# Low parts of layer 0's weights and the sums of squares on VectorE in place of GpSimd, and the first norm's products in another order

## The chip, the cores and the metric

The kernel runs on one core of one Trainium2 chip. The metric is the device time of one execution in microseconds (us); three executions of the kernel before give a median, and one further execution was profiled. The engines are named as in the profile: PE is TensorE, DVE is VectorE, ACT is ScalarE, POOL is GpSimd, SP is SyncE, which issues most DMAs.

## What is computed

A two-layer transformer block on 512 latent tokens and 256 context tokens, 1024 wide, all in float32. Layer 0 mixes with a gated linear recurrence (RG-LRU), layer 1 with a latent attention (MLA); each layer has a SwiGLU feed-forward part of hidden width 2816. Each part is entered through an RMS norm with a shift and a scale (and left through a gate) that are made from the conditioning vector.

```python
def _rmsnorm(x, g):
    y = xf * lax.rsqrt(jnp.mean(xf * xf, axis=-1, keepdims=True) + NORM_EPS)
...
def _modulate(h, shift, scale):
    return h * (1.0 + scale) + shift
...
def _swiglu(h, w_in, w_out):
    g, u = jnp.split(h @ w_in, 2, axis=-1)
    return (jax.nn.silu(g) * u) @ w_out
...
def _rglru_mixer(h_ctx, h_lat, w_in, conv_w, conv_b, gate_w, gate_b, lam, w_out, need_ctx):
    g_lat, u_lat = jnp.split(h_lat @ w_in, 2, axis=-1)
    u_lat = _dwconv_centred(u_lat, conv_w, conv_b)
    ...
    a_l, b_l = _rglru_coeffs(u_lat, gate_w[d], gate_b[d], lam[d])
    hl, _ = _linear_scan(a_l, b_l, hc_final, reverse)
    out_lat = ((y_lat[0] + y_lat[1]) * jax.nn.gelu(g_lat)) @ w_out
```

## The kernel before

**Two-part products.** Every float32 operand of a matmul is split into a high part in a rounded format and the low remainder. A product is then three matmuls, high by high, low by high and high by low (`mm3`, L791). Activations are kept transposed, features on partitions: `xT` is the residual stream, `hh` and `hl` the two parts of the normed input. `LAT` is columns 0 to 511, `CTXS` columns 512 to 767.

**The weight stream.** `Stream` brings the weights in. SP loads a raw tile of 1 or 0.5 MB (`raw`, two buffers, `NB_RAW = 2`); ACT makes the high part `wh` from it (L108), and the engine `st.low_engine` then makes the low part, `wl = raw - wh` (L119). In the code `advance` emits L108 of a unit, and emits L119 of the unit before it (`flush` emits what is left). When the last L119 of a raw tile has been emitted, `fill` emits the next load into the same buffer, so on the chip that load waits for this L119. `low_engine` is POOL from the start through the LRU, DVE in layer 0's feed-forward part, POOL from that part's last output tiles on and in the MLA, DVE in layer 1's feed-forward part and POOL for its entry.

**The start** (`START`, L38) is an order written out by hand. `h0` splits unit 0, `H` flushes, `B` and `D` turn bias rows into columns, `S`, `E` and `L` are products, evacuations and loads for the conditioning, `n` and `l` make the first norm's `nt`/`hh` (L669, L671) and `hl` (L672), `pkj` are PE's three matmuls of row k with weight unit j.

**The LRU.** For four blocks: a convolution (ACT L895, then DVE L899 twelve times for two tiles), its split (ACT `uh` L904, DVE `ul` L905), gate products on PE (`ga`), tanh on ACT (`tg` L931), the decay and scan on DVE (L941 to L964), the gated result's split (L985, L988) and the out product (`lo`). Each stage is in order on its engine. The L119 of the weights to come stand among them on POOL. POOL also issues the loads of the conditioning weights (`ada`, L242), which wait for PE.

**Boundaries.** Four times the residual is updated from PSUM by DVE (`xT`, L767) for eight row blocks m, and the sum of squares of the new `xT` is collected: ACT squares it (`sq`, L783) and POOL adds it (`acc`, L785), deferred in the list `accs`. Context columns come first, then latent columns; while the latent blocks are updated, the context blocks are normed (`nt`, `hh`, `hl`) and PE multiplies them with the next part's weights. Boundary 1 stands between LRU and feed-forward part (about 343 to 375 us), 2 before the MLA (870 to 925), 3 before layer 1's feed-forward part (1170 to 1200), 4 is the end.

Of the kernel before, what the change touches and what calls it, by code (L numbers as in the profile page):

```python
# [12 lines left out]
ALU = mybir.AluOpType  # L13
# [3 lines left out]
D = 1024  # L17
# [18 lines left out]
ENTRY_AT = (12, 6)  # L36

START = (  # L38
    "H h0 L1 S00 X S01 S02 Y B S03 E0 h1 n0 l0 n1 h2 D S10 H l1 S11 S12 p01 S13 p00 L2 p10 E1 p11 n2 "
    "l2 S20 p02 p12 C S21 n3 S22 S23 l3 p20 p21 E2 n4 p22 p31 p30 l4 p32 n5 L3 S30 l5 A S31 S32 S33 "  # L40
    "p41 E3 n6 p40 l6 p42 p52 p51 p61 n7 p50 l7 C p60 p70 h3 p71 p62 p72 H C").split()

# [19 lines left out]
class Stream:  # L62
# [3 lines left out]
    def __init__(self, nc, raw_pool, w_pool):  # L66
        self.nc, self.raw_pool, self.w_pool = nc, raw_pool, w_pool
        self.loads, self.units = [], []
        self.loaded = self.split = self.base = 0
        self.raw, self.tiles, self.freed, self.pending = {}, {}, set(), []  # L70
        self.hold = 0
        self.more = {}
        self.low_engine = nc.gpsimd

    def load(self, cols, emit):
        self.loads.append([cols, emit, 0])
# [69 lines left out]
def kernel(ctx, tc, x, c, ctx_in, c_ctx, ada_w, ada_b, norm_mix_g, norm_ffn_g, ffn_w_in,  # L146
# [3 lines left out]
    nc = tc.nc  # L150
    act, dve, pe = nc.scalar, nc.vector, nc.tensor
# [109 lines left out]
    st = Stream(nc, raw_pool, w_pool)  # L261
# [334 lines left out]
    def ada_until(l, ch):  # L596
        n = sum(1 for a in adas if a[:2] <= (l, ch)) - ada_state["used"]
        for _ in range(n):
            ada_add()
            ada_evac()  # L600
            ada_one()
        if n >= 0:
            ada_add()
            ada_evac()
# [26 lines left out]
    acc = big.tile([P, T], F32, name="acc")  # L631
# [69 lines left out]
    def boundary(last_group, na, after=lambda i: None, at=(1, 3, 2)):  # L701

        n = len(last_group)
        i0, i1, per = (0, 1, 3) if n == 4 else at
        k = 0
        act.activation(ss6[:, 0:1], ones[:, 0:1], AF.Sqrt)
        for i, f in enumerate(last_group):
            f()
            if i == i0:
                na.stats()  # L710
            if i == i1:
                na.spread()
            after(i)
            if i >= i1:
                flush_acc()
                if k < KT:
                    na.tiles(k, min(KT, k + per))
                k = min(KT, k + per)
        if k < KT:
            na.tiles(k, KT)  # L720
# [33 lines left out]
    accs = []  # L754
    sq_from, last_sq = [None], [None]

    def final_gain(m, s):
        dve.tensor_scalar(xT[:, m, s], xT[:, m, s], fin_g[:, m:m + 1], None, op0=ALU.mult)

    def flush_acc():  # L760
        while accs:
            accs.pop(0)()

    def residual(m, ps, l, ch, group, stat):

        v, s = group
        dve.scalar_tensor_tensor(xT[:, m, s], ps(s) if callable(ps) else ps[:, s], mod[:, l, ch, v, m:m + 1], xT[:, m, s],  # L767
                                 op0=ALU.mult, op1=ALU.add)
        flush_acc()
        if stat:  # L770
            at_end = l == 1 and ch == 5 and m == KT - 1 and s.start > 0
            if l == 1 and ch == 5 and not at_end:
                accs.append(lambda: final_gain(m, s))
            if m == 0:
                act.activation(acc[:, s], xT[:, m, s], AF.Square)
            else:
                sq = sq_from[0](f"sq{l}{ch}{m}{s.start}")
                if sq.shape[1] == T:
                    last_sq[0] = sq
                    sq = sq[:, s]  # L780
                else:
                    sq = sq[:, :s.stop - s.start]
                act.activation(sq, xT[:, m, s], AF.Square)  # L783
                if not at_end:
                    accs.append(lambda: nc.gpsimd.tensor_tensor(acc[:, s], acc[:, s], sq, op=ALU.add))  # L785

    def mm3(ps, wh, wl, xh, xl, parts, first, last, off=0):

# [347 lines left out]
    def ffn0(na, nb, nxt):  # L1136
        ga, gb = na.group, nb.group
        with ExitStack() as es:
# [14 lines left out]
            A, B = slice(0, H2), slice(H2, T)  # L1153
# [49 lines left out]
            def out_tile(c, m, groups, ks, ps=None):  # L1203
                h0, nh, outs = s0_out[c]
                per = 8 // nh
                wh, wl = st.get(outs[m // per])
                ps = ps or {g[0]: ps_bank(f"fo0{c}{m}{g[0]}")[:, :g[1].stop - g[1].start] for g in groups}
                for k in ks:
                    o = k * (1024 // nh) + m % per * P
                    for q, (w, x) in enumerate(((wh, ah), (wh, al), (wl, ah))):  # L1210
                        for v, s in groups:
                            pe.matmul(ps[v], w[:, o:o + P], x[:, k, s], start=k == 0 and q == 0,  # L1212
                                      stop=k == nh - 1 and q == 2)
                return ps

            def out_done(c, m):
                per = 8 // s0_out[c][1]
                if m % per == per - 1:
                    st.done(s0_out[c][2][m // per])
# [4 lines left out]
            def pair(j, i, last):  # L1224

                g = tmp.tile([P, T], F32, name=f"g0{j}", tag="nt")
                p5 = ptemp(f"p5{j}")
                y, z, x = (ps_bank(f"{c}{j}")[:, :H2] for c in "yzx")
                product(1, j, x, True, True)
                act.activation(g[:, A], x, AF.Copy)  # L1230
                while split:
                    split.pop()()
                release(1, j)
                ada_step()
                product(5, j, z, True, True)
                act.activation(p5, z, AF.Copy)
                release(5, j)
                product(6, j, x, False, True)
                act.activation(g[:, B], x, AF.Copy)
                release(6, j)  # L1240
                product(2, j, y, True, True)
                dve.tensor_tensor(g[:, A], g[:, A], y, op=ALU.add)
                act.activation(g[:, A], g[:, A], AF.Silu)
                release(2, j)
                if on_pe():
                    ada_step()
                product(7, j, x, False, True)
                dve.tensor_tensor(p5, p5, x, op=ALU.add)
                release(7, j)
                product(3, j, z, False, True)  # L1250
                dve.tensor_tensor(g[:, B], g[:, B], z, op=ALU.add)
                act.activation(g[:, B], g[:, B], AF.Silu)
                release(3, j)
                product(4, j, x, False, True)
                dve.tensor_tensor(g[:, B], g[:, B], p5, op=ALU.mult)
                dve.tensor_tensor(g[:, A], g[:, A], x, op=ALU.mult)
                if last:
                    split_hidden(i, g)
                else:
                    split.append(lambda: split_hidden(i, g))  # L1260
                release(4, j)
# [40 lines left out]
            for c, (h0, nh, outs) in enumerate(s0_out):  # L1302
                for j in range(max(h0, PLAIN0), h0 + nh):
                    pair(j, j - h0, j == h0 + nh - 1)
                lastp = c == len(s0_out) - 1
                if lastp:
                    ada_until(1, 4)
                    for m in range(KT):
                        ps = out_tile(c, m, (ga,), range(nh))
                        residual(m, lambda s: ps[1], 0, 5, ga, True)  # L1310
                        if m == 0:
                            st.flush()
                    st.low_engine = nc.gpsimd

                    def last(m):
                        ps = out_tile(c, m, (gb,), range(nh))
                        residual(m, lambda s: ps[0], 0, 5, gb, True)
                        out_done(c, m)

                    boundary([lambda m=m: last(m) for m in range(KT)], nxt, at=(1, 2, 1))  # L1320
                    return

                n0 = nh - 1 if c else 2
                three = [out_tile(c, m, (gb, ga), range(n0)) for m in range(3)]
                for m in range(KT):
                    if m < 3:
                        ps = out_tile(c, m, (gb, ga), range(n0, nh), three[m])
                    else:
                        ps = out_tile(c, m, (gb, ga), range(nh))
                    for g in (gb, ga):  # L1330
                        residual(m, lambda s: ps[g[0]], 0, 5, g, False)
                    out_done(c, m)
                    ada_step(1 if nh < 4 or on_pe() else 2)
# [3 lines left out]
    adastack.close()  # L1337
    adastack = ExitStack()
    ffn0(na, nb, na1)
    ps_layout((3, 1024))  # L1340
    adastack.close()
# [414 lines left out]
```

## Time and profile before

| what | value |
|---|---|
| three executions | 1569.62, 1568.83, 1565.91 us; median 1568.83 |
| the profiled execution | 1571.79 us, of which the span of the trace is 1569.9 |
| PE busy | 1512.2 us (96%) |
| DVE busy | 934.2 us (60%) |
| ACT busy | 675.9 us (43%) |
| POOL busy | 281.5 us (18%) |

The span runs from the first to the last instruction; what lies around it is 1.9 us. The profiled execution is 2.96 us above the median. A busy time is a sum over instructions and averages over stages with different limits: PE is busy throughout the feed-forward parts, and has gaps in the start, the LRU and at the boundaries.

### The profile page before, as it was taken

The numbers are of one execution on the slowest core, as the hardware profiler recorded it, in microseconds if no ns is written. First come the engines' busy times: TensorE is split into PE (matmuls) and PEld (weight loads), VectorE is DVE, ScalarE is ACT, GpSimd is POOL, SyncE is SP. The second block draws the span as 40 slices with busy tenths as digits, with TensorE's granted clock in tenths as the row PEclk, the third lists the DMA queues.
The fourth block names the chain that finished last, engine by engine and source line by source line (L and its number), as shares of the span: only waits on it lengthen the run. The fifth ranks groups of instructions, "written<-read, shape, count | busy, mean of one in ns | idle before, by whom it ended". The sixth has DMA issues, their size and how long they took to land.

```text
span 1569.9 us, 21629 instructions
## 1 busy us (share of the span) xinstructions
PE 1512.2 (96%) x8903; PEld 1321.4 (84%) x8903; DVE 934.2 (60%) x1397; ACT 675.9 (43%) x989; POOL 281.5 (18%) x261
## 2 busy tenths in 40 slices
PE   7999998979999999999999998999998999999998
PEld 5877876868878898999989887899998888888887
DVE  5766778686855657767587457666537543233234
ACT  5486555734423241433424343766644322232223
POOL 3223333242010101001010332111144100000002
PEclk9999999989999999999999999999999999999999
DMA  9434333131233334333242112110112433223222
GB/s 359 127 108 135 108 122 120 59 103 48 68 108 114 104 112 128 114 114 122 94 141 64 51 56 69 29 43 28 54 54 75 161 118 104 81 98 117 81 69 93
DMA packets 134995, 155.14 MB, mean 99 GB/s; under 512 B 6252, under 2 KB 112353, under 8 KB 134897
## 3 DMA queue, kind: packets, MB, share of 16 engines
q1 hardware_dynamic: 122272, 112.21, 22.3%
q0 software_dynamic: 12320, 41.02, 8.2%
q8 instruction: 70, 1.15, 0.3%
q10 hardware_dynamic: 304, 0.53, 0.1%
q14 instruction: 29, 0.23, 0.0%
HBM read 151.64 MB, written 2.10 MB: 98 GB/s over the span
## 4 chain that ended last, share of the span: by engine, by line
PE 82%; DVE 11%; ACT 4%; issue 1%; DMA 1%; SPq 0%; POOL 0%; DVEq 0%; ACTq 0%; POOLq 0%
PE f L791 14%; PE fo L1212 11%; PE x L1166 10%; PE fo L791 8%; PE z L1166 5%; PE lo L791 3%; PE s L1555 3%; PE ga L791 2%; PE wo L791 2%; PE y L1166 2%; PE o L1597 2%; PE p L791 2%; PE g L791 2%; DVE yc L899 1%; PE t L1573 1%
## 5 line engine op out<-in xcount | busy, mean ns | idle before, releaser
L108 ACT ACTIVATE wh<-raw 128x1024 fp32r<-128x1024 f32 (+3 forms) x247 | 208.5, 871 | 203.9 <-PE fo L1212 64.5
L119 POOL TENSOR_TENSOR wl<-raw,wh 128x1024 fp32r<-128x1024 f32 (+3 forms) x66 | 157.5, 2397 | 328.8 <-ACT wh L108 328.6
L119 DVE TENSOR_TENSOR wl<-raw,wh 128x1024 fp32r<-128x1024 f32 (+2 forms) x181 | 169.3, 948 | 11.8 <-ACT wh L108 11.8
L767 DVE SCALAR_TENSOR_TENSOR xT<-fo,mod,xT 128x512 f32<-128x512 f32 (+1 forms) x124 | 74.1, 626 | 129.8 <-PE fo L1212 66.2
L239 POOL DMA_DIRECT2D ada<-in_ada_w_dram x96 | 51.7, 539 | 465.3 <-PE psada L570 217.9
L791 PE MATMUL f<-hh,wh 128*128 128x512 f32 x320 | 124.7, 390 | 0.0
L791 PE MATMUL f<-hh,wl 128*128 128x512 f32 x320 | 124.5, 389 | 0.0
L791 PE MATMUL f<-hl,wh 128*128 128x512 f32 x320 | 124.5, 389 | 0.0
L785 POOL TENSOR_TENSOR acc<-acc,sq 128x256 f32<-128x256 f32 (+1 forms) x52 | 50.7, 975 | 374.1 <-ACT sq L783 371.9
L1212 PE MATMUL fo<-ah,wh 128*128 128x512 f32 (+1 forms) x352 | 98.3, 345 | 0.9 <-DVE g L1273 0.8
L1212 PE MATMUL fo<-al,wh 128*128 128x512 f32 (+1 forms) x352 | 95.8, 338 | 0.4 <-DVE al L1201 0.4
L1212 PE MATMUL fo<-ah,wl 128*128 128x512 f32 (+1 forms) x352 | 95.3, 337 | 0.0
L1109 DVE TENSOR_TENSOR sg<-sg,f 128x512 f32<-128x512 f32 x20 | 13.7, 687 | 116.4 <-ACT sg L1108 116.4
L1108 ACT ACTIVATE sg<-f 128x512 f32<-128x512 f32 x20 | 12.0, 599 | 148.3 <-PE f L791 148.3
L791 PE MATMUL fo<-ah,wh 128*128 128x512 f32 (+1 forms) x200 | 73.0, 365 | 0.0
L791 PE MATMUL fo<-ah,wl 128*128 128x512 f32 (+1 forms) x200 | 72.7, 364 | 0.0
L791 PE MATMUL fo<-al,wh 128*128 128x512 f32 (+1 forms) x200 | 72.7, 364 | 0.0
L791 PEld LDWEIGHTS f<-hh,wh 128*128 128x128 f32 x320 | 60.1, 188 | 13.2 <-issue 0.8
L791 PEld LDWEIGHTS f<-hh,wl 128*128 128x128 f32 x320 | 60.1, 188 | 12.6
L791 PEld LDWEIGHTS f<-hl,wh 128*128 128x128 f32 x320 | 60.1, 188 | 12.4
L1212 PEld LDWEIGHTS fo<-ah,wh 128*128 128x128 f32 x352 | 56.2, 188 | 12.8 <-issue 4.6
L1212 PEld LDWEIGHTS fo<-al,wh 128*128 128x128 f32 x352 | 56.2, 188 | 8.0 <-DVE al L1201 0.7
(490 smaller groups left out, 4023.3 us busy)
## 6 DMA issues: line engine op xcount, KB each, us to landing
raw<-in_ffn_w_in_dram SPq DMA_DIRECT2D x26, 1024.0 KB, 4.9
ada<-in_ada_w_dram POOLq DMA_DIRECT2D x96, 256.0 KB, 3.1
raw<-in_ffn_w_out_dram SPq DMA_DIRECT2D x19, 1024.0 KB, 4.9
raw<-in_ffn_w_in_dram SPq DMA_DIRECT2D x36, 512.0 KB, 4.7
ada<-in_ada_w_dram POOLq DMA_DIRECT2D x30, 512.0 KB, 4.4
ada<-in_ada_w_dram SPq DMA_DIRECT2D x32, 256.0 KB, 5.5
raw<-in_lru_w_in_dram SPq DMA_DIRECT2D x10, 512.0 KB, 5.3
raw<-in_lru_gate_w_dram SPq DMA_DIRECT2D x16, 256.0 KB, 3.2
```

What stands on the lines that cost most here:

```text
L108: nc.scalar.activation(dst(hi), src(self.raw[load]), AF.Copy)
L119: self.low_engine.tensor_tensor(dst(lo), src(self.raw[load]), dst(hi).bitcast(F32), op=ALU.subtract)
L239: eng.dma_start(t, ada_w[l, k * P:(k + 1) * P, c0:c0 + 512])
L767: dve.scalar_tensor_tensor(xT[:, m, s], ps(s) if callable(ps) else ps[:, s], mod[:, l, ch, v, m:m + 1], xT[:, m, s], op0=ALU.mult, op1=ALU ...
L785: accs.append(lambda: nc.gpsimd.tensor_tensor(acc[:, s], acc[:, s], sq, op=ALU.add))
L791: pe.matmul(ps[:, off + s.start:off + s.stop], a, b[:, s], start=first and i == 0, stop=last and i == 2)
L899: dve.scalar_tensor_tensor(y[:, s0:s1], ps[:, s0 + o:s1 + o], convw(tap, k), y[:, s0:s1], op0=ALU.mult, op1=ALU.add)
L1166: pe.matmul(ps, w[:, o:o + P], x[:, k0 + k, s], start=first and k == 0 and q == 0, stop=last and k == 3 and q == 2, skip_group_check=not f ...
L1212: pe.matmul(ps[v], w[:, o:o + P], x[:, k, s], start=k == 0 and q == 0, stop=k == nh - 1 and q == 2)
L1555: pe.matmul(ps[:, o:o + 384], x, y[:, k0:k1], start=j == 0, stop=j == 4)
L1573: pe.transpose(ps[:, j * P:(j + 1) * P], prs[h, b][:, j // 3, j % 3 * P:(j % 3 + 1) * P], ident)
L1597: pe.matmul(ps[:, :256], x[:, t % 4, hs], y[:, t, :], start=t == 0 and j == 0, stop=t == NT - 1 and j == 2)
```

## The change

`low_engine` starts as VectorE, so L119 of the start and of the LRU runs on DVE, and the line that set it to GpSimd for the last output tiles of layer 0's feed-forward part is gone. L785 runs on DVE in all four places. In `START` a flush stands after `Y`, and `p00` and `p01` change places. Lines after 1313 move up by two.

```diff
 START = (
-    "H h0 L1 S00 X S01 S02 Y B S03 E0 h1 n0 l0 n1 h2 D S10 H l1 S11 S12 p01 S13 p00 L2 p10 E1 p11 n2 "
+    "H h0 L1 S00 X S01 S02 Y H B S03 E0 h1 n0 l0 n1 h2 D S10 H l1 S11 S12 p00 S13 p01 L2 p10 E1 p11 n2 "
...
-        self.low_engine = nc.gpsimd
+        self.low_engine = nc.vector
...
-                    accs.append(lambda: nc.gpsimd.tensor_tensor(acc[:, s], acc[:, s], sq, op=ALU.add))
+                    accs.append(lambda: dve.tensor_tensor(acc[:, s], acc[:, s], sq, op=ALU.add))
...
                         if m == 0:
                             st.flush()
-                    st.low_engine = nc.gpsimd
-
                     def last(m):
```

In all, 37 L119 of 128x1024 and two of 128x512, and the 52 L785, pass from POOL to DVE; each keeps its place in the order of the code, and so gets a place in DVE's queue. What now stands there is shown at two places.

DVE in the LRU's third block, where the scan of the second direction (`L962`, `L964`) is followed by the convolution of the next tile (`yc`, L899) (a piece of the difference; + is new):

```order
 L962 SCALAR_TENSOR_TENSOR tg_1524<-a_1694,tg_1524 128x768
 L964 TENSOR_TENSOR tg_1330<-tg_1330,tg_1524 128x768
+L119 TENSOR_TENSOR wl_1723<-raw_1572,wh_1722 128x1024
+L119 TENSOR_TENSOR wl_1819<-raw_1726,wh_1818 128x1024
 L899 SCALAR_TENSOR_TENSOR yc_1877<-u_1_1828,cols_d,yc_1877 128x511 x2
 L899 SCALAR_TENSOR_TENSOR yc_1877<-u_1_1828,cols_d,yc_1877 128x510
```

Two low parts now stand between L964 and the convolution `yc_1877`; and the buffer of `raw_1572` comes free for its next load only after L964.

DVE in boundary 1, where latent blocks of `xT` are updated from the out product `lo` and context blocks are normed (`nt`, `hl`):

```order
 L767 SCALAR_TENSOR_TENSOR xT<-lo_4_3090,mod,xT 128x512
+L785 TENSOR_TENSOR acc<-acc,sq_3098 128x512
 L669 SCALAR_TENSOR_TENSOR nt_2_512_3101<-xT,gm,R_f0a 128x256
 L672 SCALAR_TENSOR_TENSOR hl_79<-nt_1_512_3086,mod,hh_78 128x256
 L767 SCALAR_TENSOR_TENSOR xT<-lo_5_3105,mod,xT 128x512
+L785 TENSOR_TENSOR acc<-acc,sq_3113 128x512
 L669 SCALAR_TENSOR_TENSOR nt_3_512_3116<-xT,gm,R_f0a 128x256
 L672 SCALAR_TENSOR_TENSOR hl_79<-nt_2_512_3101,mod,hh_78 128x256
```

The sum for a latent block stands right behind the update of the same block, and ahead of `nt` and `hl`; its operand `sq` is made by ACT from that update.

## Rows read from the trace of the kernel before

**Rows 1.** The page's first part: the span and each engine's busy time, share and instructions

```profile
span 1569.9 us, 21629 instructions
...
PE 1512.2 (96%) x8903; PEld 1321.4 (84%) x8903; DVE 934.2 (60%) x1397; ACT 675.9 (43%) x989; POOL 281.5 (18%) x261
```

**Rows 2.** Windows by stage: LRU, then boundaries 1 and 3; busy time, PE clock, DMA share, GB/s

```profile
62.00:343.00 281.00, 259.99 (x1575) 213.34 (x1574) 198.13 (x214) 170.63 (x184) 95.59 (x60) 0.96 0.36 113
343.00:375.00 32.00, 29.22 (x174) 25.52 (x173) 24.64 (x46) 16.13 (x31) 16.63 (x18) 0.95 0.28 91
1170.00:1200.00 30.00, 25.98 (x207) 25.05 (x206) 20.81 (x37) 14.47 (x29) 23.39 (x22) 0.99 0.34 112
```

**Rows 3.** What PE waited for from 62 to 343: us, times, longest

```profile
PE lo L791 <- DVE xT L767: 8.2, 1, 8.2
PE ga L791 <- DVE yc L899: 5.1, 1, 5.1
PE lo L791 <- ACT tg L931: 3.0, 1, 3.0
PE ga L791 <- ACT uh L904: 3.0, 1, 3.0
PE ga L791 <- ACT tg L931: 1.4, 1, 1.4
```

**Rows 4.** Groups of instructions by form: busy us, mean ns of one, idle before and releaser

```profile
L119 POOL TENSOR_TENSOR wl<-raw,wh 128x1024 fp32r<-128x1024 f32 x56 | 142.6, 2552 | 217.4 <-ACT wh L108 217.1
...
L119 DVE TENSOR_TENSOR wl<-raw,wh 128x1024 fp32r<-128x1024 f32 x83 | 100.0, 1226 | 2.6 <-ACT wh L108 2.6
...
L785 POOL TENSOR_TENSOR acc<-acc,sq 128x256 f32<-128x256 f32 (+1 forms) x52 | 50.7, 975 | 374.1 <-ACT sq L783 371.9
...
L767 DVE SCALAR_TENSOR_TENSOR xT<-fo,mod,xT 128x512 f32<-128x512 f32 x68 | 50.9, 749 | 116.0 <-PE fo L1212 59.9 <-PE fo L791 56.1
...
L767 DVE SCALAR_TENSOR_TENSOR xT<-fo,mod,xT 128x256 f32<-128x256 f32 x56 | 26.7, 477 | 13.8 <-PE fo L791 7.3 <-PE fo L1212 6.3
```

**Rows 5.** DVE and POOL in the LRU: start, duration, instruction

```profile
265.46 3.60 DVE L964 TENSOR_TENSOR tg<-tg,tg 128x768 f32<-128x768 f32 x1
...
309.62 3.84 DVE L962 TENSOR_TENSOR_SCAN tg<-a,tg 128x768 f32<-128x768 f32 x1
...
322.31 1.76 DVE L962 TENSOR_TENSOR_SCAN tg<-a,tg 128x768 f32<-128x768 f32 x1
...
308.93 6.73 POOL L119 TENSOR_TENSOR wl<-raw,wh 128x1024 fp32r<-128x1024 f32 x2 [14.16 <-ACT wh L108]
```

**Rows 6.** PE after its longest wait in the LRU

```profile
326.97 0.85 PE L791 MATMUL lo<-ml,wh 128*128 128x512 f32 x2
```

**Rows 7.** SP, ACT, DVE and PE around 200

```profile
190.38 0.37 SPq L268 DMA_DIRECT2D raw<-in_lru_w_out_dram  x1
...
195.69 0.99 ACT L895 ACTIVATE yc<-u,cols_d 128x768 f32<-128x768 f32 x1
...
196.69 2.97 DVE L964 TENSOR_TENSOR tg<-tg,tg 128x768 f32<-128x768 f32 x1
...
205.73 0.51 PE L791 MATMUL ga<-ul,wh 128*128 128x512 f32 x2
```

**Rows 8.** DVE and SP where the start passes into the LRU

```profile
61.30 7.41 DVE L899 SCALAR_TENSOR_TENSOR yc<-p,cols_d,yc 128x511 f32<-128x511 f32 x12 [0.39 <-issue]
...
64.40 1.06 SPq L288 DMA_DIRECT2D raw<-in_lru_gate_w_dram  x2
```

**Rows 9.** DVE and ACT in boundary 1

```profile
355.11 0.75 DVE L767 SCALAR_TENSOR_TENSOR xT<-lo,mod,xT 128x512 f32<-128x512 f32 x1
...
360.10 0.74 DVE L767 SCALAR_TENSOR_TENSOR xT<-lo,mod,xT 128x512 f32<-128x512 f32 x1
...
357.75 0.63 ACT L783 ACTIVATE sq<-xT 128x512 f32<-128x512 f32 x1 [0.35 <-DVE xT L767]
```

**Rows 10.** DVE in boundary 3

```profile
1187.40 2.56 DVE L672 SCALAR_TENSOR_TENSOR hl<-nt,mod,hh 128x256 fp32r<-128x256 f32 x1
```

## The prediction

> **What bounds the kernel now.** The engine totals come first: PE is busy 1512.2 of 1569.9 us, DVE 934.2, POOL 281.5 [rows 1]. PE is the bound over the whole, so a change of other engines can only touch the 58 us in which PE stands, and what it loses at its lower clock behind a long stand. So the windows by stage come next: in the LRU PE is busy 260.0 of 281 us, in boundary 1 29.2 of 32, in boundary 3 26.0 of 30 [rows 2]. Both feed-forward parts are left out, since PE does not stand there and the moved work isn't there. The waits of PE then say who is late: of the 21 us in the LRU, 8.2, 5.1, 3.0, 3.0 and 1.4 are ended by DVE or by an ACT step behind DVE [rows 3]. None is ended by POOL. So POOL's own 2.55 us for a low part, twice DVE's 1.23 [rows 4], is no cost in itself. Last, DVE's timeline tells why DVE is late: the same scan L962 takes 1.76 us at 322.31 and 3.84 at 309.62, and the second one runs inside two L119 of POOL (308.93, 6.73 for both); L964 at 265.46 takes 3.60 [rows 5]. A DVE operation with two inputs in SBUF that meets a running POOL L119 ends about when that does. I count 19 such operations between 91 and 317 us, at about 2 us each, by their lengths above those of unheld ones: 38 us of DVE time. The convolutions (L899) read PSUM and are not held: twelve take 7.41 at 61.30 [rows 8].
>
> After a long stand PE is slow as well: behind the 8.2 us a pair of matmuls takes 0.85 us [rows 6], where a pair takes 0.51 at 205.73 [rows 7].
>
> **What the change removes and adds.** On DVE the moved low parts cost 34 x 1.13 = 38 us in the start and the LRU (1.23 is one instruction alone; two back to back take 2.35 in the trace's groups, so 1.13 is the step). What is removed is also 38 us of holding, plus some 4 in the start. DVE's total barely moves; what counts is the place of each.
>
> *Price of L785 on DVE.* No row shows it. The nearest rows are L767, with as many elements: 0.75 us for 128x512, 0.48 for 128x256 [rows 4]; next to each other they step by some 0.66 and 0.39. I take the steps; the bounds are these and the full durations. [...]
>
> *The start.* `nt` is held no more (-2 on DVE), and `p00` first lets PE begin earlier. But the low part behind the convolutions now waits for DVE until about 68.7 (61.30 + 7.41), and the load of its buffer, which SP issues at 64.40 [rows 8], with it; ACT's next high part is queued in front of a tanh. Early gain and late loss of about 1.5 each: 0.
>
> *The 3.0 us wait for uh (130.06).* On the chain before it four and a half holds of 2.1 go (-9.4); three low parts enter (+3.4). The wait and the slow clock (about 1.7) hold only 4.7 us, and a load that is released later by DVE (111.27 before) takes up to 1 of it: -3.9, between -2 and -5.
>
> *A low part for the u product near 177.* It now stands behind held work's old place: +0.6, from 0 to 1.
>
> *The 3.0 us wait for tg (212.75).* Here L964 at 196.69 loses its hold of 2 us [rows 7], and the gelu product behind it 2.6; two low parts enter (the first piece of the order) for +2.3. But the load that SP issues at 190.38 [rows 7] is released by the first of them, so now at about 198.8 instead of 190.35. With the 4.2 us of such a load it lands at 203; the high part made from it stands on ACT ahead of the convolution's first step, which starts at 195.69 now and would start at 204. The next gate product, near 205.7 [rows 7], then waits to about 210: a new stall of 4.7 in place of one of 3.0. I take +2, between -4 and +5.
>
> *The 1.4 us wait (237.52)*: two holds go, no low part enters: -1.4. *The 5.1 us wait (272.87)*: holds at 257.93 and 265.46 go, -4.7 [rows 5]; two low parts enter, +2.3; with the slow clock: -3, between -2.4 and -3.9.
>
> *The 8.2 us wait (326.17) and boundary 1 go together*, as PE meets the same chain. The three holds at 309.62, 313.50 and 317.38 (-6.1) and two earlier (-3.4) go, two low parts enter (+2.3): the products `lo` begin 7.2 us earlier. Then in boundary 1, DVE does for a latent block `xT`, `nt` and `hl` (0.66 + 0.39 + 0.39 = 1.44), and 355.11 to 360.10 is three blocks in 4.99, or 1.66 each [rows 9]. L785 now stands right behind `xT`, and must wait for ACT's `sq` of the same block (0.63, [rows 9]; 0.75 with what passes between). That is 0.66 + 0.75 + 0.66 + 0.39 + 0.39 = 2.85 a block. With five low parts that enter from the third lo tile on, less what PE already waits for, the last `hl` comes 6.1 us later after the start of `lo` (3 to 8). Together -1.1 (-4 to +1).
>
> *Boundary 2* has the same order, with more PE work for each block, which covers DVE's 2.85; three low parts and two halves enter, three holds of `hl` go: +0.4 (-1.5 to +1.5). *Boundary 3* has latent halves of 256 (0.39 for L785, 0.42 for `sq` and its passing): 2.1 a block on DVE against PE's 1.4. And here POOL still makes four low parts, which hold `hl` today (2.56 instead of 0.48 at 1187.40 [rows 10]): +2.5 (+1 to +5). The end has spare DVE time: 0.
>
> Sum: -3.9 + 0.6 + 2 - 1.4 - 3 - 1.1 + 0.4 + 2.5 = **-3.9 us**. The profiled execution of 1571.8 becomes 1567.9; it stood 2.96 above the median, so the median of 1568.8 becomes **1565**. What a measurement tells from no change is 0.3%, or 4.7 us: the forecast lies just inside.
>
> **Rivals.** *The LRU is freed altogether* (A): the loads are not late enough to be felt. Then the wait at 212.75 gives 3.5 instead of costing 2, the lo start gives its slow clock too (3.1), and boundary 1 costs 3 in place of 6.1: -3.9 - 5.5 - 3.1 - 3.1 = -15.6, 1553. For it: ACT and DVE have gaps in the LRU (170.6 and 198.1 of 281 busy [rows 2]). Against it: two raw buffers alone carry the stream.
>
> *The boundaries take more than the LRU gives* (B), slower: the wait of L785 for `sq` is paid by each of eight latent blocks in full, 8 x 1.4 = 11.2 at boundary 1 and 5 at boundary 3. That is 5.1 and 2.5 beyond the sum: +3.7; with the low parts of boundary 2 no longer covered (+1.1), +4.8, 1573.6. It decides once PE's own work on a block is much shorter than 2.85 us on DVE in both. Against it: PE has some slack in boundary 1, where `hl` came early.
>
> *Late raw loads* (C): the chain of L119, load and high part that I find at 198.8 exists also at 68 and 116. If each costs 3 more than taken: +9 on three places, 1574. The gap in SP's issues would show it.
>
> *L785 is held as well* (D). Rows show POOL's L119 holding DVE operations with two SBUF inputs [rows 5, 10]; `acc` and `sq` are two, and four L119 remain on POOL at boundary 3. If each holds an acc beyond what it holds today, 4 x 2 = 8 less what the stall covers, about +4: 1569. [...]
>
> *Nothing is felt* (E): DVE's work just changes places, 1568.
>
> **How the numbers follow.** Forecast with its own spread (1561 to 1570) 0.40; A 0.23; B 0.14; C 0.09; D 0.08; E 0.06. A and the better part of the forecast lie beyond -4.7 us: faster 0.23 + 0.19 = 0.42. B and two thirds of C lie beyond +4.7, and part of a wider mishap in D and the forecast: slower 0.14 + 0.06 + 0.05 = 0.25. The rest, 0.33, is within 0.3%. The range goes from A's time to 3 us beyond B and C, since those can come together: 1553 to 1577.
>
> **What would show it.** In the profile after: L962 at 1.76 and L964 at 0.96 in all eight places; the waits near 272 and 326 down to under 3 and 2; SP's load of the out weights later, and a wait of ACT's L895 near 200; in boundary 1 `acc` on DVE waiting 0.75 for ACT, and a longer wait of PE for `hl`. Wrong would be: L785 that doesn't wait for `sq`; waits of DVE for something else in the LRU; PE standing in the feed-forward parts, where nothing was moved.

## The result and the profile after

The changed kernel takes 1592.78 us (median of four), the kernel before 1569.22 beside it: a ratio of 1.0153, 95% interval 1.0122 to 1.0184, so 1.5% slower, where 1565 with a range of 1553 to 1577 was forecast. The profiled execution took 1596.62.

The page of the changed kernel, first part:

```profile
span 1594.9 us, 21562 instructions
...
PE 1519.4 (95%) x8903; PEld 1324.1 (83%) x8903; DVE 947.7 (59%) x1488; ACT 678.5 (43%) x989; POOL 131.6 (8%) x170
```

DVE's total rose by 13.5 us only (934.2 before [rows 1]), little, as forecast; POOL's fell by 150. PE's busy time rose by 7: the same matmuls, some of them at a lower clock (the mean granted clock is 0.981, before 0.985). So the 25 us of span are 18 of standing and 7 of slowness, and the place has to be found. The two kernels issue their matmuls in the same order (but for `p00` and `p01`), so the k-th matmul of one trace can be set against the k-th of the other. Start before, start after, and the shift, worked out from the two traces:

```
first gate product (ga)               70.18   70.14   -0.0
ga behind the wait of 3.0 for uh      130.06  132.04   +2.0
u, third block                        178.18  181.82   +3.6
g, third block                        196.18  202.72   +6.5
lo behind the wait of 3.0 for tg      212.75  219.07   +6.3
ga, third block, second direction     229.56  236.89   +7.3
lo, second block, second half         248.72  263.38  +14.7
ga behind the wait of 5.1             272.87  284.45  +11.6
g, fourth block                       303.95  323.45  +19.5
lo behind the wait of 8.2             326.17  339.98  +13.8
f00g, the first of boundary 1         358.90  379.63  +20.7
ckv, the first of boundary 2          908.81  934.78  +26.0
v, behind boundary 2                  969.91  991.27  +21.4
f10g, the first of boundary 3        1188.74 1212.29  +23.6
```

All of it is lost in the LRU and at the boundaries, and in between the shift stays. Where PE has just waited, the first start does not yet hold the slow matmuls behind the wait (pairs of 1.01 and then 0.84 us in place of 0.51, behind the longest of them at 323.45); sizes of steps below are read where the shift stays again. The windows by stage, with bounds moved to where the same matmuls now lie, answer to [rows 2] (LRU, boundaries 1 and 3; busy time of PE, PEld, DVE, ACT, POOL, then PE's clock, DMA share, GB/s):

```profile
62.00:361.00 299.00, 266.28 (x1577) 217.28 (x1576) 192.95 (x243) 171.32 (x184) 16.93 (x32) 0.94 0.35 109
361.00:399.00 38.00, 31.91 (x173) 27.49 (x173) 28.58 (x60) 17.00 (x30) 0.00 (x0) 0.88 0.17 56
1191.00:1224.00 33.00, 28.05 (x206) 26.87 (x205) 25.49 (x47) 14.96 (x30) 13.30 (x8) 0.90 0.30 99
```

The LRU takes 299 us in place of 281, with PE standing 33 in place of 21. In boundary 1 the clock is 0.88 (0.95 before). What PE waited for from 62 to 361 answers to [rows 3]:

```profile
PE g L791 <- DVE wl L119: 12.4, 2, 10.0
PE lo L791 <- DVE wl L119: 7.2, 1, 7.2
PE ga L791 <- ACT uh L904: 4.6, 1, 4.6
PE lo L791 <- DVE xT L767: 4.2, 3, 1.9
PE ga L791 <- DVE wl L119: 2.2, 1, 2.2
PE lo L791 <- ACT tg L931: 1.2, 1, 1.2
PE u L791 <- DVE wl L119: 0.5, 1, 0.5
```

The waits of 8.2 and 5.1 are gone, and in their place stand four kinds of waits for something that no row of before names: a low part, `wl`, made by DVE. They sum to 22.3 us.

The groups by form show what was removed and what was bounded from L767's rows [rows 4, 5]:

```profile
L962 DVE TENSOR_TENSOR_SCAN tg<-a,tg 128x768 f32<-128x768 f32 x8 | 14.1, 1756 | 0.3
...
L785 DVE TENSOR_TENSOR acc<-acc,sq 128x256 f32<-128x256 f32 x35 | 20.3, 579 | 4.1 <-ACT sq L783 4.1
...
L785 DVE TENSOR_TENSOR acc<-acc,sq 128x512 f32<-128x512 f32 x17 | 11.7, 690 | 7.7 <-ACT sq L783 7.7
```

L962 takes 1.756 in all eight places, where POOL had held it to a mean of 2.54: the holds are gone. L785 on DVE is 0.69 for 512 columns, between the two bounds of 0.66 and 0.75. For 256 columns the mean of 0.58 includes four that POOL still holds at boundary 3; the others take 0.41 to 0.43.

**Where the low parts stand.** The longest wait, in the timeline of ACT, DVE and PE:

```profile
299.75 1.04 ACT L108 ACTIVATE wh<-raw 128x1024 fp32r<-128x1024 f32 x1
...
305.66 0.96 DVE L951 SCALAR_TENSOR_TENSOR tg<-b,tg 128x768 f32<-128x768 f32 x1 [3.08 <-ACT tg L950]
...
310.57 0.96 DVE L951 SCALAR_TENSOR_TENSOR tg<-b,tg 128x768 f32<-128x768 f32 x1 [3.08 <-ACT tg L950]
...
320.99 1.28 DVE L959 TENSOR_TENSOR_SCAN tg<-a,tg 128x512 f32<-128x512 f32 x1
...
322.19 2.34 DVE L119 TENSOR_TENSOR wl<-raw,wh 128x1024 fp32r<-128x1024 f32 x2
...
323.45 1.01 PE L791 MATMUL g<-hh,wl 128*128 128x512 f32 x2 [9.96 <-DVE wl L119]
```

The high part of unit 27 (counted in the order of the stream) is made at 299.75. Its low part takes 1.2 us but stands on DVE behind 13 operations of the decay and the scan, four of which wait for ACT, and runs at 322.19. PE, which could have gone on at some 313.5, starts at 323.45, at half speed (granted clock 0.50; 1.01 for the first pair). Before, POOL made the same low part 1.14 us behind the start of its high part:

```profile
291.23 1.05 ACT L108 ACTIVATE wh<-raw 128x1024 fp32r<-128x1024 f32 x1
...
292.37 2.40 POOL L119 TENSOR_TENSOR wl<-raw,wh 128x1024 fp32r<-128x1024 f32 x1
```

The rule of the code is the reason: `advance` emits a low part only when the next unit's turn comes, which in the written order can be many DVE operations later. For POOL, which has little else in its queue, a late place in the code costs next to nothing (in experiment 10 an earlier place gains at most 0.2%); for DVE it is a late time.

**What a late low part holds up beside PE.** DVE, POOL, SP, ACT and PE near 120:

```profile
116.63 1.22 DVE L119 TENSOR_TENSOR wl<-raw,wh 128x1024 fp32r<-128x1024 f32 x1
...
117.59 1.05 POOL L242 DMA_DIRECT2D ada<-in_ada_w_dram  x2 [8.61 <-PE psada L570]
...
117.93 0.37 SPq L268 DMA_DIRECT2D raw<-in_lru_w_in_dram  x1
...
125.33 1.06 ACT L108 ACTIVATE wh<-raw 128x1024 fp32r<-128x1024 f32 x1 [8.65 <-DMA raw<-in_lru_w_in_dram]
...
126.29 0.98 ACT L895 ACTIVATE yc<-u,cols_d 128x768 f32<-128x768 f32 x1
...
132.04 1.01 PE L791 MATMUL ga<-uh,wh 128*128 128x512 f32 x2 [4.60 <-ACT uh L904]
```

The low part at 116.63 frees a raw buffer; the load follows at 117.93 (111.27 before) and the high part made from it waits for it 8.65 us, with the convolution's first step (L895) behind it on ACT. This is the chain that the prediction has at 116 and 199, and called rival C. The load itself has become longer, since it now meets the two loads of conditioning weights (`ada`) that POOL issues at 117.59 and 118.11. Issue to landing, in the change and then before:

```profile
raw<-in_lru_w_in_dram SPq DMA_DIRECT2D x1, 512.0 KB, 7.4
...
raw<-in_lru_w_in_dram SPq DMA_DIRECT2D x1, 512.0 KB, 3.7
```

So `uh` comes 2 us later than before in place of 4 earlier.

**Boundary 1** on DVE, answering to [rows 9]:

```profile
375.83 0.75 DVE L767 SCALAR_TENSOR_TENSOR xT<-lo,mod,xT 128x512 f32<-128x512 f32 x1
377.34 0.69 DVE L785 TENSOR_TENSOR acc<-acc,sq 128x512 f32<-128x512 f32 x1 [0.76 <-ACT sq L783]
377.95 0.47 DVE L669 SCALAR_TENSOR_TENSOR nt<-xT,gm,R_f0a 128x256 f32<-128x256 f32 x1
378.34 0.48 DVE L672 SCALAR_TENSOR_TENSOR hl<-nt,mod,hh 128x256 fp32r<-128x256 f32 x1
378.73 0.75 DVE L767 SCALAR_TENSOR_TENSOR xT<-lo,mod,xT 128x512 f32<-128x512 f32 x1
380.24 0.69 DVE L785 TENSOR_TENSOR acc<-acc,sq 128x512 f32<-128x512 f32 x1 [0.76 <-ACT sq L783]
```

Each block has `xT`, a wait of 0.76 for ACT's square, the sum, `nt` and `hl`: 375.83 to 378.73 is 2.90 a block, against 2.85 worked out.

### The profile page after: what moved, and what is told of

Read it like the earlier page. It is cut to its first block, busy times and chain, and to the rows that moved or that the text cites. A ratio compares the mean times of both kernels' runs of the same rounds, so it can differ in the third digit from the quotient of the medians.

```text
span 1594.9 us, 21562 instructions
## 1 busy us (share of the span) xinstructions
PE 1519.4 (95%) x8903; PEld 1324.1 (83%) x8903; DVE 947.7 (59%) x1488; ACT 678.5 (43%) x989; POOL 131.6 (8%) x170
## 4 chain that ended last, share of the span: by engine, by line
PE 79%; DVE 10%; ACT 6%; DMA 3%; issue 1%; SPq 0%; DVEq 0%; ACTq 0%
PE f L791 14%; PE fo L1212 11%; PE x L1166 9%; PE fo L791 8%; PE z L1166 5%; PE s L1553 3%; PE lo L791 3%; PE y L1166 2%; PE wo L791 2%; PE o L1595 2%; PE ga L791 2%; DMA raw<-in_lru_w_in_dram 2%; DVE yc L899 2%; PE u L791 2%; DVE wl L119 1%; PE p L791 1%
## 5 line engine op out<-in xcount | busy, mean ns | idle before, releaser
L119 DVE TENSOR_TENSOR wl<-raw,wh 128x1024 fp32r<-128x1024 f32 (+2 forms) x220 | 214.1, 985 | 19.4 <-ACT wh L108 19.2
L767 DVE SCALAR_TENSOR_TENSOR xT<-fo,mod,xT 128x512 f32<-128x512 f32 (+1 forms) x124 | 74.1, 626 | 122.4 <-PE fo L791 62.6
L119 POOL TENSOR_TENSOR wl<-raw,wh 128x1024 fp32r<-128x1024 f32 (+2 forms) x27 | 57.9, 2163 | 320.5 <-ACT wh L108 320.5
L1212 PEld LDWEIGHTS fo<-ah,wh 128*128 128x128 f32 x352 | 56.2, 188 | 12.8 <-issue 4.6
L1212 PEld LDWEIGHTS fo<-ah,wl 128*128 128x128 f32 x352 | 56.3, 189 | 7.9
```

The lines of the kernel that those rows point to most:

```text
L119: self.low_engine.tensor_tensor(dst(lo), src(self.raw[load]), dst(hi).bitcast(F32), op=ALU.subtract)
```

## Experiments

Each was timed beside runs of the kernel before; ratios are to that kernel.

**1. The low parts alone.**

```diff
-                    accs.append(lambda: dve.tensor_tensor(acc[:, s], acc[:, s], sq, op=ALU.add))
+                    accs.append(lambda: nc.gpsimd.tensor_tensor(acc[:, s], acc[:, s], sq, op=ALU.add))
```

> The change without its second part: L785 on POOL again, low parts of layer 0 and the order of the start as in the change. Theory (low parts that PE waits for stand late in DVE's queue in the LRU): most of the loss stays, since the five waits of PE for wl lie before any sum: about 1586 us, 17 above the kernel before, and the last f00g of boundary 1 some 20 us late. Rival (the sums on DVE, which wait for ACT, carry it): the loss falls to under 8 us, 1577 or less.

Measured: 1587.86 (1.0116, 1.0092 to 1.0139), +19 us. The shift at the g product of the fourth block is 19.0, against 19.5 in the change. Most of the loss lies ahead of any sum.

**2. The sums alone** (on the kernel before, the same line the other way).

> The kernel before with L785 alone on DVE. Theory: the sums cost 3 to 6 us at boundary 1 and about 2.7 at boundary 3, and give some back at boundary 2: 1573, +4 (+1 to +8). Rival (sums carry the loss): +15 or more, 1584.

Measured: 1579.74 (1.0070, 1.0044 to 1.0096), +10.8. Neither forecast: more than 8, less than 15. Matmul against matmul, the shift grows by 3.6 in boundary 1, 3.1 in boundary 2, 3.6 in boundary 3 and 1.4 at the end (11.7; the 3.3 that this one trace gained in the LRU are left out, where the trace of experiment 3 gained 3.9 with an unchanged median). PE's first waits in boundary 1 (340 to 375):

```profile
PE f01g L791 <- DVE xT L767: 2.2, 1, 2.2
PE f00g L791 <- DVE xT L767: 1.3, 1, 1.3
```

Beside the late low parts the same sums cost 4.9 only (1592.8 against 1587.9).

**3. The order of the start alone** (the two `START` edits on the kernel before).

> The kernel before with the order of the start alone changed (the flush after Y, p00 before p01). Both theories: within 2 us of the kernel before; PE begins its first norm's products up to 2 us earlier, and loses that again before the first gate product.

Measured: 1568.39 (1.0001, 0.9984 to 1.0017). Nothing, as forecast.

**4. Five low parts back on POOL.**

```diff
-        self.low_engine.tensor_tensor(dst(lo), src(self.raw[load]), dst(hi).bitcast(F32), op=ALU.subtract)
+        eng = self.nc.gpsimd if i in (15, 17, 20, 23, 27) else self.low_engine
+        eng.tensor_tensor(dst(lo), src(self.raw[load]), dst(hi).bitcast(F32), op=ALU.subtract)
```

> The change with the low parts of five of the 34 units of the start and the LRU (15, 17, 20, 23, 27 in the order of the stream) on POOL again: those for which PE waits in the trace of the change. Theory (they stand behind scans in DVE's queue): the steps of 0.9, 3.8, 2.8, 9 and 12.3 us at these five places go, what waited there anyway comes back in part (the two later ones gave back 6.6 and 11): 1592.8 less about 12, 1581 (1576 to 1585). Rival (raw loads that are released late, or high parts on ACT): PE waits for the next unit instead, and less than 4 us are gained: 1589 or more.

Measured: 1569.63 (1.0003, 0.9989 to 1.0018): 23 us come back with five operations of 1.2 us. That is twice the forecast: what had stood at the same places in the kernel before does not come back in full. The other 29 low parts, off POOL, no longer hold DVE (all eight scans L962, here L963, take 1.76). Its lo products begin 13.0 us ahead of the kernel before (313.21 against 326.17). PE's longest waits from 62 to 325:

```profile
PE lo L792 <- DVE wl L120: 4.0, 1, 4.0
PE ga L792 <- ACT uh L905: 2.7, 1, 2.7
PE lo L792 <- DVE xT L768: 1.8, 1, 1.8
```

**5. Those five, and the sums, back on POOL.**

> The run with five low parts back on POOL, and L785 back on POOL as well; the other 32 low parts stay on DVE. Theory (DVE freed of POOL's holds in the LRU, low parts that PE waits for not on DVE, boundaries as before): its LRU comes to the lo products of boundary 1 some 15 us early, and boundary 1 gives back less than the 9 us that it did with the sums on DVE: 1561, -8 against the kernel before (-5 to -12). Rival (the early arrival is lost at boundary 1 anyway, on what else stands there): 1567 or more.

Measured: 1561.03 (0.9943, 0.9927 to 0.9959), -7.5, as forecast, though its lo products begin 10.2 us early and not 15.

**6. Four further low parts on POOL** (units 29, 31, 32, 33 added to the five of the run before).

> As the run before, with four further low parts on POOL: unit 29, for which PE waited 4.0 us in the first such run, and 31 to 33, which stand on DVE ahead of the context blocks of boundary 1. Theory: 2 to 5 us less than the run before, 1558. Rival (POOL holds DVE's last scans again, as in the kernel before): 0 to 4 us more.

Measured: 1562.70 (0.9969, 0.9954 to 0.9984). The intervals overlap those of experiment 5 a little, and it is no gain. The rival's number came, but not its reason: all eight scans take 1.76, so POOL holds none of them. The first two waits of PE from 62 to 345 say what stands there:

```profile
PE lo L792 <- DVE wl L120: 5.9, 1, 5.9
PE cst_f0a L649 <- POOL acc L786: 4.5, 1, 4.5
```

A wait for a low part is still there, and POOL, now with low parts in front of the sums, makes PE wait 4.5 for a sum.

**7. The sums on DVE, one block later** (on the kernel of experiment 2).

```diff
             if i >= i1:
-                flush_acc()
                 if k < KT:
```

> The kernel before with L785 on DVE, but emitted behind the update of the next block, where ACT's square has long been made (the flush in the boundary's loop is left out). With L785 right behind its own block the same kernel was 10.8 us slower than before. If it is the wait for ACT's square (0.75 a block, 8 blocks, three boundaries), most of it goes: 1572, +3. If it is the time of 24 more operations on DVE, ahead of nt and hl: 1577, +8 or more.

Measured: 1584.63 (1.0099, 1.0083 to 1.0114), 4.9 more than experiment 2. The wait for the square is not what costs, or is not all of it. PE's waits in boundary 1 now (340 to 380):

```profile
PE cst_f0b L648 <- DVE acc L784: 2.2, 1, 2.2
PE f00g L790 <- DVE hl L672: 1.7, 1, 1.7
...
PE f01g L790 <- DVE xT L766: 1.2, 1, 1.2
```

The wait for `xT` in boundary 1 falls, but a new wait of 2.2 for the last sum itself has come, in front of the latent columns' statistics; the shift grows by 5.8 in boundary 1 in place of 3.6. So the edit took one wait away and made another, and doesn't price the square's wait cleanly.

**8. All low parts on DVE, emitted earlier.**

```diff
+    since = 9
     for op, *f in STEPS:
         n, *f = map(int, f or "0")
+        if op not in "wa":
+            since += 1
+            if since == 3:
+                st.flush()
+        if op == "w":
+            since = 0
         if op in "ug":
```

> The change, with each low part of the LRU emitted at the latest three steps behind its high part (of the written order, not counting the steps w and a) in place of at the next unit's turn: the five that PE waits for stand 16, 3, 8, 7 and 13 DVE operations earlier. All on DVE. Theory (place in DVE's queue, not the engine): 10 to 18 us of the loss go, 1578. Rival (it needs a second engine): under 5 us, 1588 or more.

Measured: 1560.65 (0.9946, 0.9931 to 0.9960): 32 us less than the change, 8 less than the kernel before, with the same operations on the same engines. Unit 27 in ACT's, DVE's and PE's timelines:

```profile
277.11 1.04 ACT L108 ACTIVATE wh<-raw 128x1024 fp32r<-128x1024 f32 x1
...
278.19 1.23 DVE L119 TENSOR_TENSOR wl<-raw,wh 128x1024 fp32r<-128x1024 f32 x1 [0.77 <-ACT wh L108]
...
290.69 0.51 PE L791 MATMUL g<-hh,wl 128*128 128x512 f32 x2
```

Its low part starts 1.08 us behind the start of its high part, 44 us ahead of where it stood, and PE's product, at 323.45 in the change, starts at 290.69 without a wait. The first two waits of PE from 62 to 325:

```profile
PE lo L791 <- DVE wl L119: 2.8, 2, 2.0
PE lo L791 <- DVE xT L767: 2.1, 3, 0.9
```

The gate product at 130.06 of the kernel before starts at 126.08 here, 4 us early: the load behind unit 9 is early too (issued at 110.82, behind one pair of conditioning loads and ahead of the next, it took 3.8).

**9. The same, with the sums on POOL.**

> The run with all low parts of the LRU on DVE, emitted three steps behind their high parts, with L785 back on POOL. Theory (the sums on DVE cost 7 to 11 us at the boundaries and the end, as they did alone and beside late low parts 5): 1552, -16 against the kernel before (-11 to -19). Rival (the 20 us by which the lo products come early are lost at boundary 1 on something else): 1558 or more.

Measured: 1550.46 (0.9894, 0.9878 to 0.9911), 18 us less than the kernel before. Its page:

```profile
span 1546.9 us, 21607 instructions
...
PE 1505.0 (97%) x8903; PEld 1314.0 (85%) x8903; DVE 931.1 (60%) x1436; ACT 676.6 (44%) x989; POOL 181.6 (12%) x222
```

PE's standing is 42 us, 16 less than in the kernel before, and its busy time is 7 less; the 18 us by which the lo products come early survive boundary 1 (-18.1 at the first lo, -17.9 at the first ckv).

**10. The kernel before, with the earlier place** (all on POOL).

> The kernel before, low parts and sums on POOL, with the same earlier place of the low parts in the written order. Theory (POOL makes a low part as soon as its high part is there, whatever its place, so the place matters on DVE alone): 1568, within 4 us of the kernel before. Rival (the earlier place itself is what gains, on any engine): 1560 or less.

Measured: 1565.99 (0.9988, 0.9978 to 0.9998): a gain of at most 0.2%. The group of L962 shows that POOL still holds it:

```profile
L962 DVE TENSOR_TENSOR_SCAN tg<-a,tg 128x768 f32<-128x768 f32 x8 | 22.8, 2849 | 0.3
```

So the earlier place matters on DVE. With the low parts at the same places, those of the LRU on DVE (experiment 9) are worth 15.5 us more than on POOL. The freedom from the holds is the likely cause: DVE's other operations in the LRU take 34 us less in sum, and PE's two longest waits, 7.8 and 4.1 in this run and ended by DVE, are down to 0.7 each there. That a low part itself takes 1.2 us in place of 2.4, and frees its raw buffer sooner, is in the same difference and was not tested apart.

## Why the prediction was wrong

**The failed step** is the inventory of the moved low parts. The prediction asked of each what it delays behind it on DVE and when its raw buffer comes free, and for one only ("A low part for the u product near 177": +0.6; measured +0.9) when PE needs it. It put all others at the cost of their time. Four more are needed by PE before DVE comes to them: the shift rises by 4.2 (g, 196), 4.0 (ga, 229), 9.4 (lo, 248) and 12.8 (g, 304), slow clock included. The low parts of these five places start 11 to 23 us behind the start of their high parts, so no load is missing there. Experiment 4 shows that these five low parts carry the loss; experiment 8, that their place in DVE's queue does, and not the engine. Since both also free raw buffers earlier, what the late loads cost apart from the waits for `wl` is not separated; at 130 the trace shows such a load by itself.

The medians give the sizes: low parts on DVE at an early place -18 (experiment 9), the sums on DVE +10 on top of that (8 against 9), the late place +32 (the change against 8). The prediction's terms up to the lo products sum to -12.9 and those of the boundaries to +9.0, near the first two; the third it did not have.

**The holds** were right. 38 was worked out, and DVE's other operations that started between 62 and 343 take 39.1 less in sum. L962 is at 1.756 everywhere; experiments 4, 5, 8 and 9 bring the lo products 10 to 18 us forward, where the terms up to there have 12.9 (one trace against one; that of experiment 3 is 3.6 ahead there by itself). One reading was off, without a change of the price. Before:

```profile
118.39 2.40 POOL L119 TENSOR_TENSOR wl<-raw,wh 128x1024 fp32r<-128x1024 f32 x1
...
118.55 3.87 DVE L962 TENSOR_TENSOR_SCAN tg<-a,tg 128x768 f32<-128x768 f32 x1
```

The held scan does not end with the low part, at 120.79, but 1.63 behind it: it runs nearly its whole 1.76 after it.

The other terms, each with the slow clock behind its wait:

- **The start**, 0: right (0.0 at the first gate product; -1.4 in the trace of experiment 8, whose start is the same; experiment 3 changes nothing).
- **130, -3.9**: measured +2.4 (+0.3 to +2.7). The chain was seen, but the load was mis-sized: its delay was let cost up to 1, and beside the conditioning loads it took 7.4 in place of 3.7, with ACT's convolution behind it. Experiments 1, 4, 5 and 6 have the same low parts up to here: loads of 8.0, 5.8, 7.6 and 5.4 go with +3.1, +0.7, +2.4 and -0.6. With the load early (experiment 8) it is -4.8.
- **212, +2**: measured -3.3 (+8.1 to +4.8), and -2.9 in experiment 8. The chain is there and later than worked out (the load at 202.73 for 198.8, L895 at 207.50 for 204). But the new stall of 4.7 didn't come at the gate product, which PE reached 8.1 late, held up by unit 17.
- **237, -1.4; 272, -3**: measured -1.7 and -7.2, the latter against a delay of 9.4 just before it, so that it tests little.
- **326 and boundary 1, -1.1**: from +22.2 (last steps of the g product) to +23.8 behind boundary 1: +1.6; in experiment 8, -1.1. The block price of 2.85 was right (2.90), but PE waits there for `xT` (2.2 and 1.3, as in experiment 2), and for `hl` no longer than before (1.3, before 1.8).
- **Boundary 2, +0.4**: -1.5 in the change, +1.1 in experiment 8, but not for the reason given. The sums alone cost 3.1 there, so PE's work didn't cover DVE's 2.85 a block; with the low parts moved and the sums on POOL, the boundary gives back 1.9 (experiment 9) to 3.4 (experiment 1).
- **Boundary 3, +2.5**: +2.0 in the change and in experiment 8; the sums alone cost 3.6. **The end**, 0: 1.4, as PE waits for the last sum.

**The rivals.** A's time was reached only with the low parts early and the sums on POOL (experiment 9, 1550.5 for 1553); with the sums on DVE it is 1560.7. B had the sign but not the place: the sums alone cost 10.8, a third of it in boundary 1. C had the right cause, a late L119 on DVE, and followed it to the buffer and the load, and not to PE. D (a held sum at boundary 3) took place: four sums of 256 columns there take 2.12, 2.04, 1.60 and 1.57 us beside four of POOL's last five low parts, where the others take 0.41 to 0.43. Above the others' 0.42 that is 5.7 us of DVE time; DVE's other operations there take 5.5 less than before, and boundary 3 cost no more than the sum had. The range ended at 1577; the measured time is 16 us above it.

Most of what the prediction named as signs came true: L962 at 1.76 and L964 at 0.96 in all eight places, no more waits of 5.1 and 8.2, the late load of the out weights, `acc` waiting 0.76 for ACT. None of these signs looks at PE waiting for a low part.

## What to carry to other kernels

When work moves from an engine with an empty queue to one with a full queue, write down for each moved operation when its consumer needs it, and where the new queue stands by then; a place in the code that was harmless on the idle engine becomes a time. If the trade is good in total, as here (holds against added time), then move the operation in the written order as well: five late ones of 34 cost 23 us, and the same change with an earlier flush gained 8 against the kernel before.

## What was not expected of the hardware

Five operations of 1.2 us on DVE were worth 23 us of the program's time (experiment 4). Behind each wait for a low part of 2.2 to 10 us PE ran matmul pairs at 0.84 in place of 0.51 or 0.52. For unit 27 the granted clock (behind the busy times) was 0.50 until 328.90:

```profile
323.45:328.90 5.45, 5.45 (x17) 4.68 (x18) 4.66 (x4) 1.63 (x3) 0.00 (x0) 0.50 0.55 192
328.90:331.00 2.10, 2.10 (x14) 1.85 (x13) 0.00 (x0) 1.80 (x2) 0.00 (x0) 0.97 0.00 0
```

Behind the waits of 0.5 and 1.2 it was 1.00.

The same raw load of 0.5 MB took 3.7 to 3.8 us from issue to landing where SP issued it some 3 us behind a pair of POOL's conditioning loads (seven traces, that of before among them). It took 5.4 and 5.8 where it was issued 0.1 us or less ahead of such a pair (experiments 6 and 4), and 7.4 to 8.0 between the two or just behind both (the change, experiments 5 and 1).
